# Value weights in tiles of their own, their loads spread over four products, and all refilled low parts on VectorE, in a hybrid attention and retention block

## The chip, the cores and the metric

The kernel runs on one core of one Trainium2 chip, in one launch. The metric is the device time of that core in microseconds (us). TensorE is called PE here, VectorE DVE, ScalarE ACT, GpSimd POOL and SyncE SP. Before the change the median of three runs is 1945.7 us (1945.29 to 1947.35).

## The reference, cut to what matters

A sequence of 2048 rows of 1024 numbers goes through one block. All is computed to float32 accuracy.

```python
h = rms_norm(x, norm_gain[l])
proj = jnp.einsum('bsd,df->bsf', h, w_in[l])
q_a, k_a, v_a, g_a, q_r, k_r, v_r, g_r, m_a, m_r = split_columns(proj)
o_a = chunk_band_attention(q_a, k_a, v_a, rel_bias[l])        # 8 heads, own chunk of 64 and 8 before it
branch_a = jnp.einsum('bsf,fd->bsd', o_a * jax.nn.silu(g_a), w_out_attn[l])
o_r = retention_chunkwise(rotary(q_r), rotary(k_r), v_r, gn_gain[l])   # 8 heads, decay by head
branch_r = jnp.einsum('bsf,fd->bsd', o_r * jax.nn.silu(g_r), w_out_ret[l])
mixed = jax.nn.sigmoid(m_a) * branch_a + jax.nn.sigmoid(m_r) * branch_r
x = x + jnp.einsum('bsd,de->bse', mixed, w_out[l])
return rms_norm(x, final_gain)
```

The change touches the first two lines: the normalized rows, and their product with `w_in`, for the values `v_a` and `v_r` above all.

## The kernel before, in words

**Arithmetic.** Each float32 operand of a matmul is held as two tiles: a high part, which ACT casts (`act.copy`, CAST in the profile), and a low part, the operand less the high part, which DVE or POOL subtracts (TENSOR_TENSOR). A product is then three passes: high by high, high by low, low by high. In the projections, seven products of quarters stand for eight (Strassen's scheme in Winograd's form): `PRODUCTS` lists them with the weight operand (`b11` to `b22`, or a sum `t1` to `t4` of them) and the PSUM bank (x, y, v, z, w). The operands on the side of the rows, `R[0]` to `R[6]` (tile r in the profile, high and low), are made once for each half of the sequence and stay in SBUF.

**Stages.** The sequence is worked in two halves of 1024 rows. Job p0 projects queries, keys and values of the first half (span 0 to about 320 us), in chunks of 256 columns, numbered 0 to 10; g0 projects the gates and fills PE in attention and retention of the first half (to about 750). `reload` then refills R for the second half from DRAM (`cscr`, cs in the profile), where `second_half` has put its parts during p0; p1 does the same chunks (about 755 to 1060), g1 fills attention and retention again (to 1500), and the output projections follow.

**The three kinds of chunk.** `Strassen` has a product of 12 matmuls of 128x512, in four steps of three; the weights are the moving or the stationary operand by the chunk. `Rows` (chunks 3, 5 and 10: values) gives rows by columns, and has 14 half products of 24 matmuls of 128x256, also four steps each. `Front` is the start of p0.

**What sets the order.** The program is written out in one order, which each engine keeps. `dense` yields one step (three matmuls, or six of half size) at a time; `later(n, fn)` puts work n steps later; `prime` prepares an item (a product or a half product) three items ahead: ACT casts the high part (`wh`), and four steps later DVE makes the low part (`wl`). `RAW_LEADS` says how many items ahead of a chunk its weights are loaded: nine and eight. The loads are issued on ACT's queue, in order with ACT's casts. For a `Rows` chunk, line 456 `load(self, js)` issues two loads of 512 KB at lead nine, and four of 256 KB at lead eight, all four in a row.

**Tiles.** `E` gives a tile of 128x512 from one ring (line 113), of 23 tiles in the projections (`E_PROJ`), in program order; it serves projected keys, queries and values until they are put to DRAM, rows of the second half, and in `Rows` the lower weights and `t2`. `raw` is a ring of three tiles of 512 KB for weights. `C` and `t` are rings for sums.

**Other places of the change.** `piece` in `second_half` fetches rows of the second half (xs), scales them on ACT (line 927), and six steps later has PE transpose them (`turn`, tile pst); ACT then scales the transposed tile by the gain, and sums of such tiles go to `cscr`. Line 1154 has PE transpose the keys of the retention (tile trkr_k), fifteen steps after a product's end and more. `refill` (line 974) loads one tile of R's low side with the full number, ACT casts the high part from it, and DVE or POOL subtracts in place; `reload` gives every third of the 28 to POOL:

```python
later(1, lambda k=k, t=t: refill(m, k, cscr[m][k], 8 + 2 * t - 4 * at, pool if t % 3 == 2 else dve))
```

## Time and profile before

| | us |
|---|---|
| median of three runs | 1945.7 (1945.29 to 1947.35) |
| profiled execution | 1943.98 |
| its span | 1942.2 |
| mean granted clock of PE | 0.994 |
| PE busy | 1887.3 (97%) |
| DVE busy | 1355.7 (70%) |
| ACT busy | 930.9 (48%) |
| POOL busy | 898.4 (46%) |

The profile is of one execution. A time line has the start in us from the span's start, the length in us, the engine, the operation, the tiles written and read, and in brackets the idle time ahead of it with what ended it. ACTq is ACT's issuing of transfers. A view by windows has, for each stretch, its length, and busy time (with the number of instructions) of PE, of the weight loads of PE, DVE, ACT and POOL, then PE's granted clock, the share of the DMA engines and GB/s. A line of waits has the tile, what it waited for, the sum in us, how often, and the longest. A line of a tile's view has the number of instructions and the shortest, median and longest in ns. The buffer numbers are left out of tile names. PE's busy time is the quantity that the sum of all matmuls sets; its idle time, and the stretches in which the granted clock is about half, are what else makes up the span.

### The profile page before, as it was taken

What the parts mean: (1) busy time and instruction counts of PE and PEld (TensorE: products, weight loads), DVE (VectorE), ACT (ScalarE), POOL (GpSimd) and SP (SyncE); (2) the same over time, 40 slices, a digit from 0 to 9 for tenths busy, and PEclk for the clock granted to TensorE, in tenths of its full rate; (3) what the DMA queues carried; (4) which work ended last, traced back from release to release, by engine and by line L of the source; (5) the groups of instructions that cost most, each with busy time, mean ns of one, the idle gap of its engine ahead of it and who ended that gap; (6) DMA issues with size and microseconds to landing.
All of it is one profiled execution on the core that took longest, in us unless ns stands there. A gap on an engine that the chain in (4) does not pass through costs nothing. (4 is left out here: it accounts for less than half of the span.)

```text
span 1942.2 us, 31900 instructions
## 1 busy us (share of the span) xinstructions
PE 1887.3 (97%) x10437; PEld 1617.8 (83%) x10437; DVE 1355.7 (70%) x2521; ACT 930.9 (48%) x1931; POOL 898.4 (46%) x742
## 2 busy tenths in 40 slices
PE   7999999999999999999999999999999999999998
PEld 6899879888888887899879888888888878887886
DVE  6969788677756558879788677765555654547665
ACT  7544553666654545343333666664455321223554
POOL 0313525545545566323415544544564114557775
PEclk9999999999999999999999999999999999999999
DMA  6586876565559978575666555555998999977673
GB/s 195 169 279 194 255 263 217 182 192 177 175 156 277 270 239 298 186 257 187 196 222 209 158 166 174 160 155 160 272 274 269 313 357 330 320 261 237 208 240 127
DMA packets 325750, 435.93 MB, mean 224 GB/s; under 512 B 30073, under 2 KB 191377, under 8 KB 325585
## 3 DMA queue, kind: packets, MB, share of 16 engines
q1 hardware_dynamic: 260096, 368.35, 59.3%
q10 hardware_dynamic: 65488, 65.55, 11.2%
q8 instruction: 83, 1.36, 0.3%
q14 instruction: 83, 0.67, 0.1%
HBM read 288.14 MB, written 145.64 MB: 223 GB/s over the span
## 5 line engine op out<-in xcount | busy, mean ns | idle before, releaser
L142 POOL TENSOR_SCALAR pr<-pr,rsum 128x640 f32<-128x640 f32 (+4 forms) x128 | 96.5, 754 | 212.2 <-DVE ptl L142 99.8
L142 PE MATMUL ps_g_z<-r,wh_g 128*128 128x512 f32 x448 | 144.0, 403 | 1.4 <-DVE c_g L142 1.4
L142 PE MATMUL ps_g_x<-r,wh_g 128*128 128x512 f32 x448 | 143.2, 401 | 1.0 <-ACT u_g L142 0.8
L142 DVE CUSTOM_DVE_ANT_0 pr<-wide,bt 128x640 f32<-128x640 f32 (+4 forms) x128 | 94.3, 737 | 61.8 <-PE wide L142 49.7
L142 ACT ACTIVATE pr<-pr,mn 128x640 f32<-128x640 f32 (+4 forms) x128 | 98.0, 766 | 81.9 <-DVE mn L142 81.9
L142 DVE TENSOR_TENSOR ptl<-tp,pth 128x384 fp32r<-128x384 f32 x168 | 96.1, 573 | 41.2 <-ACT pth L142 37.9
L142 ACT CAST pth<-tp 128x384 fp32r<-128x384 f32 x168 | 84.5, 515 | 68.0 <-PE tp L142 64.8
L142 POOL TENSOR_TENSOR l_vr<-vrt,h_vr 128x512 fp32r<-128x512 f32 x32 | 46.8, 1463 | 121.0 <-DMA qrs<-l_q 81.3
L142 POOL TENSOR_TENSOR sl<-sm,sh 128x384 fp32r<-128x384 f32 x64 | 68.9, 1077 | 70.5 <-ACT sh L142 48.2
L142 PEld LDWEIGHTS tp<-ident,pr 128*128 128x128 f32 x560 | 71.1, 140 | 27.4 <-POOL pr L142 2.9
L142 DVE TENSOR_TENSOR sm<-sr,dm 128x384 f32<-128x384 f32 x64 | 35.6, 556 | 82.8 <-DMA dm<-in_dmask_dram 26.3
L142 POOL TENSOR_TENSOR wl_g<-t_g,wh_g 128x512 fp32r<-128x512 f32 x56 | 75.0, 1340 | 39.5 <-ACT wh_g L142 39.2
L142 PE MATMUL po<-pth,va 128*128 128x256 f32 x336 | 92.5, 296 | 0.0
L142 PE MATMUL tp<-ident,pr 128*128 128x128 f32 x560 | 89.3, 272 | 2.9 <-POOL pr L142 1.7
L142 ACT CAST wh_p<-raw_p 128x512 fp32r<-128x512 f32 x99 | 61.3, 621 | 61.7 <-PE ps_p_y L142 23.3
L142 PE MATMUL wide<-ka,qa 128*128 128x384 f32 (+1 forms) x448 | 88.3, 313 | 2.3 <-DVE mn L142 2.1
L142 PEld LDWEIGHTS wide<-ka,qa 128*128 128x128 f32 x448 | 74.5, 188 | 18.9 <-DVE mn L142 9.0
L142 PE MATMUL po<-ptl,va 128*128 128x256 f32 x336 | 88.3, 284 | 1.4
L142 PE MATMUL ps_g_z<-r,wl_g 128*128 128x512 f32 x224 | 88.3, 394 | 0.0
L142 PE MATMUL ps_g_x<-r,wl_g 128*128 128x512 f32 x224 | 88.1, 393 | 0.0
L142 DVE TENSOR_TENSOR wl_p<-raw_p,wh_p 128x512 fp32r<-128x512 f32 x99 | 82.4, 836 | 5.4 <-ACT wh_p L142 5.4
L142 POOL TENSOR_TENSOR t_g<-raw_g,t_g 128x512 f32<-128x512 f32 x56 | 73.7, 1316 | 24.6 <-DVE wl_g L142 10.6
(933 smaller groups left out, 6263.0 us busy)
## 6 DMA issues: line engine op xcount, KB each, us to landing
raw_g<-in_w_in_dram ACTq DMA_DIRECT2D x56, 512.0 KB, 4.3
raw_p<-in_w_in_dram ACTq DMA_DIRECT2D x38, 512.0 KB, 5.8
qa<-qas SPq DMA_DIRECT2D x128, 128.0 KB, 3.1
qr<-qrs SPq DMA_DIRECT2D x128, 128.0 KB, 4.6
vr<-vrs SPq DMA_DIRECT2D x64, 256.0 KB, 5.9
ka<-kas SPq DMA_DIRECT2D x56, 256.0 KB, 3.4
va<-vas SPq DMA_DIRECT2D x40, 256.0 KB, 3.3
kds<-kdt_k SPq DMA_DIRECT2D x32, 256.0 KB, 3.3
```

The lines of the kernel that those rows point to most:

```text
L142: return tc.keep_in_program_order(op(*a, **k))
```

## The change

1. `Rows.load` issues four loads of 512 KB, one each at leads 8, 7, 6 and 5 (`ROW_LEADS`), in the order b12, b11, b22, b21. The lower two go to tiles of a new tag `late` (two of them), for which the ring E has 19 tiles in place of 23: the SBUF taken is the same.
2. The sums of a `Rows` chunk are written over weight tiles: t1 over b11, t3 over b12, t4 over b21; t2 takes a tile of the ring t, so no sum takes an E tile. t1, t2 and t3 are made one item later.
3. At the start, the lower weights of chunk 1 lie in one late tile, s3 is written over a11, and s2 gets E tiles.
4. Rows of the second half are transposed eight steps after their scaling in place of six, the sums made of them two steps later; the keys of the retention are transposed three steps later.
5. All 28 low parts of the refill are made on DVE (19 before).

```diff
-E_PROJ = 23
+E_PROJ = 19
+ROW_LEADS = (8, 7, 6, 5)
@@ Rows
-            for j in range(2) if js is None else js:
-                for h in range(2):
-                    src = w_cols(w_in, self.job.cols[self.c] + T * h, 2, j)
-                    name = f"raw_{self.job.name}_{self.c}_{j}{h}"
-                    if j == 0:
-                        raw = wp.tile([P, 4, T], F32, tag="raw", bufs=RAWS, name=name)
-                        act.dma_start(raw, src)
-                        bs = [raw[:, 2 * kk:2 * kk + 2] for kk in range(2)]
-                    else:
-                        bs = [E(f"{name}_{kk}", shape=(P, 2, T)) for kk in range(2)]
-                        for kk in range(2):
-                            act.dma_start(bs[kk], src[:, 2 * kk:2 * kk + 2])
-                    self.b[f"b{j + 1}{h + 1}"] = bs
-                self.raw.append(j)
-        SUMS_AFTER = {0: ("t1", "t2", 0), 1: ("t1", "t2", 1), 2: ("t3", 0), 3: ("t3", 1), 6: ("t4", 0), 7: ("t4", 1)}
+            for j in range(4) if js is None else js:
+                k, h = ((0, 1), (0, 0), (1, 1), (1, 0))[j]
+                name = f"raw_{self.job.name}_{self.c}_{k}{h}"
+                if k:
+                    raw = epool[0].tile([P, 4, T], F32, tag="late", bufs=2, name=name)
+                else:
+                    raw = wp.tile([P, 4, T], F32, tag="raw", bufs=RAWS, name=name)
+                act.dma_start(raw, w_cols(w_in, self.job.cols[self.c] + T * h, 2, k))
+                self.b[f"b{k + 1}{h + 1}"] = [raw[:, 2 * kk:2 * kk + 2] for kk in range(2)]
+                self.raw.append(raw)
+        SUMS_AFTER = {1: ("t1", "t2", 0), 2: ("t1", "t2", 1), 3: ("t3", 0), 4: ("t3", 1), 6: ("t4", 0), 7: ("t4", 1)}
...
+            into = {"t1": "b11", "t3": "b12", "t4": "b21"}
...
@@ start_up
-        for i in range(2):
-            ch[1].b[f"b2{i + 1}"] = E(f"b2{i + 1}", shape=(P, 4, P))
+        lower = epool[0].tile([P, 4, T], F32, tag="late", bufs=2, name="lower")
+        ch[1].b.update({"b21": lower[:, :, left], "b22": lower[:, :, right]})
-        s3 = [E(f"s3_{k}") for k in range(4)]
+        s3 = a11
-        s2, s1, s4 = a11, a21, a12
+        s2, s1, s4 = [E(f"s2_{k}") for k in range(4)], a21, a12
@@ second_half
-                later(6, lambda: turn(i, f))
+                later(8, lambda: turn(i, f))
-            later(24, first)
-            later(28, second)
-            later(32, third)
+            later(26, first)
+            later(30, second)
+            later(34, third)
@@ refill
-        later(lag + 2, lambda: (low or dve).tensor_tensor(wl, r32(wl), r32(wh), ALU.subtract))
+        later(lag + 2, lambda: dve.tensor_tensor(wl, r32(wl), r32(wh), ALU.subtract))
@@ keys of the retention
-            later(late + 15 + 4 * u, lambda u=u: turn(u))
+            later(late + 18 + 4 * u, lambda u=u: turn(u))
```

On ACT, ahead of chunk 10 of p1: before, two loads and, two instructions later, four in a row (raw_p_10 are the weights of chunk 10, wh_p_9 and h_qa work of chunks 9 and 8, kdt_k of the keys).

```order
L142 ACTIVATE h_qa_2_11972<-ps_p_8_x 128x512
L142 DMA raw_p_10_00_11977<-in_w_in_dram 128x4x256
L142 DMA raw_p_10_01_11979<-in_w_in_dram 128x4x256
L142 CAST wh_p_9_4_11981<-t_p_9_11870 128x512
L142 ACTIVATE h_qa_2_12011<-u_p_8_11933 128x512
L142 DMA raw_p_10_10_0_12014<-in_w_in_dram 128x2x256
L142 DMA raw_p_10_10_1_12015<-in_w_in_dram 128x2x256
L142 DMA raw_p_10_11_0_12018<-in_w_in_dram 128x2x256
L142 DMA raw_p_10_11_1_12019<-in_w_in_dram 128x2x256
L142 CAST wh_p_9_1_12022<-t_p_9_11872 128x512
```

And with the change:

```order
L143 DMA raw_p_10_01_11973<-in_w_in_dram 128x4x256
L143 CAST wh_p_9_1_11975<-t_p_9_11841 128x512
L143 ACTIVATE h_qa_3_12006<-u_p_8_11809 128x512
L143 DMA raw_p_10_00_12009<-in_w_in_dram 128x4x256
L143 CAST wh_p_9_2_12011<-t_p_9_11866 128x512
L143 CAST kdt_k_2_0_0_12019<-trkr_k_2_0_11991 128x4x64
L143 CAST kdt_k_2_0_1_12026<-trkr_k_2_0_11991 128x4x64
L143 COPY u_p_9_12040<-ps_p_9_x 128x512
L143 DMA raw_p_10_11_12046<-in_w_in_dram 128x4x256
L143 CAST wh_p_9_3_12048<-raw_p_9_1_11765 128x512
```

Each load now stands ahead of one cast of chunk 9, and the next load behind that cast.

On PE, in the last product of chunk 8 of p0 (pst are the transposes of scaled rows xs, trkr_k those of the keys, ps_p_8_z the product), before:

```order
L142 MATMUL trkr_k_0_0_3261<-ident,u_p_7_2865 128x128
L142 MATMUL ps_p_8_z<-r_92,wh_p_8_6_3133 128x512
L142 MATMUL ps_p_8_z<-r_93,wh_p_8_6_3133 128x512
L142 MATMUL ps_p_8_z<-r_92,wl_p_8_6_3134 128x512
L142 MATMUL pst_0_1_3290<-ident,xs_0_1_3121 128x128 x4
```

And with the change:

```order
L143 MATMUL ps_p_8_z<-r_93,wh_p_8_6_3113 128x512
L143 MATMUL ps_p_8_z<-r_92,wl_p_8_6_3114 128x512
L143 MATMUL trkr_k_0_0_3267<-ident,xk_0_0_2967 128x128
L143 MATMUL trkr_k_0_0_3267<-ident,u_p_7_2846 128x128
...
L143 MATMUL pst_0_1_3274<-ident,xs_0_1_3103 128x128 x4
L143 MATMUL ps_p_8_z<-r_92,wh_p_8_6_3113 128x512
```

Before, the transposes stand behind the first step of this product; now behind the third, and the keys' transposes, which stood ahead of the product, stand directly ahead of them.

On DVE, at the start of the refill (r are the low parts, c_g_13 a sum of the last chunk of g0, wl_p weights of p1), before:

```order
L142 TENSOR_TENSOR u_g_13_9476<-ps_g_13_v,u_g_13_9384 128x512
L142 TENSOR_TENSOR r_81<-r_81,r_80 128x512
L142 TENSOR_TENSOR wl_g_13_6_9453<-raw_g_13_1_8964,wh_g_13_6_9452 128x512
L142 TENSOR_TENSOR c_g_13_9519<-ps_g_13_z,u_g_13_9476 128x512
L142 TENSOR_TENSOR r_81<-r_81,r_80 128x512
L142 TENSOR_TENSOR wl_p_0_0_9502<-raw_p_0_0_9310,wh_p_0_0_9501 128x512
```

And with the change:

```order
L143 TENSOR_TENSOR r_81<-r_81,r_80 128x512
L143 TENSOR_TENSOR wl_g_13_6_9434<-raw_g_13_1_8945,wh_g_13_6_9433 128x512
L143 TENSOR_TENSOR r_81<-r_81,r_80 128x512
L143 TENSOR_TENSOR c_g_13_9500<-ps_g_13_z,u_g_13_9457 128x512
L143 TENSOR_TENSOR r_81<-r_81,r_80 128x512
L143 TENSOR_TENSOR wl_p_0_0_9483<-raw_p_0_0_9291,wh_p_0_0_9482 128x512
```

The row of r_81 between wl_g_13_6 and c_g_13 is new here; POOL made that low part before. The other eight come in behind, two or more in a row between the low parts of the weights.

## The prediction

> **What bounds the kernel now.** I read first the page's busy times, then PE's waits, then the time lines of the engines that PE waited for.

> ```profile
> span 1942.2 us, 31900 instructions
> PE 1887.3 (97%) x10437; PEld 1617.8 (83%) x10437; DVE 1355.7 (70%) x2521; ACT 930.9 (48%) x1931; POOL 898.4 (46%) x742
> ```

> PE is busy for 1887.3 of 1942.2 us, and the change takes no matmul away. So it can win only from the 54.9 us in which PE stands still, and from time in which PE is busy at a slower clock. The waits (tile, releaser, sum, times, longest) that the change touches are these:

> ```profile
> PE ps_p_y L142 <- ACT wh_p L142: 4.7, 3, 2.8
> PE pst L142 <- ACT xs L142: 2.1, 2, 1.6
> PE ps_g_z L142 <- DVE c_g L142: 1.4, 1, 1.4
> PE ps_p_w L142 <- DVE wl_p L142: 1.4, 2, 1.0
> PE ps_p_z L142 <- DVE wl_p L142: 0.5, 1, 0.5
> PE ps_p_v L142 <- DVE wl_p L142: 0.5, 1, 0.5
> ```

> The view by windows shows the second kind of loss: its PEclk column (the 0.58, 0.57 and 1.00 ahead of the DMA share) says that the clock fell to about half in three of these stretches.

> ```profile
> 254.00:258.00 4.00, 4.00 (x15) 3.08 (x14) 2.99 (x4) 1.04 (x2) 2.96 (x2) 0.58 1.02 339
> 977.00:981.00 4.00, 3.81 (x9) 2.75 (x10) 4.00 (x7) 2.95 (x6) 1.98 (x2) 0.58 0.71 200
> 991.00:995.00 4.00, 4.00 (x11) 2.94 (x10) 3.43 (x8) 3.22 (x8) 0.00 (x0) 0.57 1.06 371
> 781.00:793.00 12.00, 10.09 (x43) 7.38 (x42) 12.00 (x13) 2.89 (x6) 8.52 (x6) 1.00 0.16 56
> ```

> **Part A, the loads of the value weights.** ACT issues them and also casts the weights, in one order. Three bursts of loads hold a cast back (ACTq is the issuing):

> ```profile
> 126.84 6.82 ACTq L142 DMA_DIRECT2D raw_p<-in_w_in_dram  x3
> 133.71 0.62 ACT L142 CAST wh_p<-t_p 128x512 fp32r<-128x512 f32 x1 [8.91 <-DMA raw_p<-in_w_in_dram]
> 254.60 8.78 ACTq L142 DMA_DIRECT2D raw_p<-in_w_in_dram  x4
> 263.42 0.62 ACT L142 CAST wh_p<-t_p 128x512 fp32r<-128x512 f32 x1 [8.38 <-DMA cs<-xs]
> 984.27 5.64 ACTq L142 DMA_DIRECT2D raw_p<-in_w_in_dram  x4
> 989.95 0.62 ACT L142 CAST wh_p<-t_p 128x512 fp32r<-128x512 f32 x1 [7.23 <-DMA raw_p<-in_w_in_dram]
> ```

> Each cast is released by a transfer, after 7.2 to 8.9 us in which ACT did nothing. PE takes up the product at once after the cast:

> ```profile
> 134.38 0.73 PE L142 MATMUL ps_p_y<-r,wh_p 128*128 128x512 f32 x2 [1.20 <-ACT wh_p L142]
> 136.21 0.62 PE L142 MATMUL ps_p_y<-r,wh_p 128*128 128x512 f32 x2
> 136.90 0.62 PE L142 MATMUL ps_p_y<-r,wh_p 128*128 128x512 f32 x2
> 137.60 0.61 PE L142 MATMUL ps_p_v<-r,wh_p 128*128 128x512 f32 x2
> 264.09 0.73 PE L142 MATMUL ps_p_y<-r,wh_p 128*128 128x512 f32 x2 [0.71 <-ACT wh_p L142]
> 267.28 0.61 PE L142 MATMUL ps_p_v<-r,wh_p 128*128 128x512 f32 x2
> 990.62 0.73 PE L142 MATMUL ps_p_y<-r,wh_p 128*128 128x512 f32 x2 [2.76 <-ACT wh_p L142]
> 995.28 0.62 PE L142 MATMUL ps_p_v<-r,wh_p 128*128 128x512 f32 x2
> ```

> A step of three matmuls takes 0.69 us (136.21 to 136.90), so a product of four steps 2.76. The three delayed products take 3.22, 3.19 and 4.66. The loss is wait plus excess, and for the second also the 0.5 of ps_p_v on wl_p, whose low part followed the late cast: 1.20 + 0.46 = 1.7; 0.71 + 0.43 + 0.50 = 1.6; 2.76 + 1.90 = 4.7, where the excess is the half clock. Together **8.0 us**.

> After the change each Rows chunk has four loads of 512 KB, one in every four steps, with casts between them, instead of two and then four in a row. The lead of the casts is three times four steps, 3 x 2.76 = 8.3 us: a single blocked load costs PE nothing until it holds ACT that long. From the landing times, a load may still find its semaphore unfired:

> ```profile
> raw_p<-in_w_in_dram ACTq DMA_DIRECT2D x2, 512.0 KB, 5.7
> krs<-h_k SPq DMA_DIRECT2D x2, 256.0 KB, 6.9
> ```

> The transfers that a load waits for land 5.7 to 6.9 us after their issue (window 975 to 992), below 8.3 but not far below, and ACT has other casts to do. So I take the three waits as gone (-8.0) and leave one new wait of the size of the first, +1.7; the bounds for what remains are 0 (no wait) and 8.0 (all three as before).

> The smaller pieces here: 24 loads in place of 36 in all; the sums t1, t2 and t3 one half product (four steps) later on DVE, still one ahead of their cast, which itself runs three ahead; three of the four sums written over a weight tile. None lies on the path as long as the lead of 8.3 us holds; if it goes, the price is that of a wait above. In the start the low half of chunk 1's weights gets a tile of its own, and s3 is written over a11: I put +0.1 there, between 0 and 0.3.

> **Part B, transposes two steps later.** In the first half PE reaches the transposes of scaled rows before ACT is done with them:

> ```profile
> 252.12 0.62 PE L142 MATMUL pst<-ident,xs 128*128 128x128 f32 x2 [1.63 <-ACT xs L142]
> 253.56 0.85 PE L142 MATMUL ps_p_z<-r,wh_p 128*128 128x512 f32 x2
> 257.19 0.38 PE L142 MATMUL trkr_k<-ident,xk 128*128 128x128 f32 x1
> 252.73 0.69 ACT L142 ACTIVATE xs<-xs,rs 128x128 f32<-128x128 f32 x2
> ```

> Between 252.12 - 1.63 = 250.5 and 253.56 PE did four short transposes, and the three steps from 253.56 took 3.63 us instead of 3 x 0.69 = 2.07, at the clock of 0.58 shown above. Now two of these steps stand ahead of the transposes, so PE gets there at 250.5 + 2 x 0.69 = 251.9. ACT ends the last scaling at 252.73 + 0.69 = 253.4 as it is; one more cast now stands ahead of it, about 0.3, so 253.7. With the transposes PE is through at about 253.9, one step is left, and the place of 257.19 is reached at about 254.6: a gain of **2.6**, which I take as 2.5. If the clock falls all the same, the 1.56 of excess stays and the gain is 0.9; if nothing waits, it is up to 4.2. The other fifteen groups of transposes (four pieces of four tiles) stand in no wait of the list, and lie two steps later at no cost.

> The keys' transposes three steps later touch the third slow stretch, which starts with a wait on c_p:

> ```profile
> 977.13 0.78 PE L142 MATMUL ps_p_z<-r,wh_p 128*128 128x512 f32 x2 [1.20 <-DVE c_p L142]
> ```

> DVE is busy in all of 977 to 981 and behind with c_p; the change takes none of the work ahead of c_p away. I take **0**, with a gain of 2 (half a clock for four us) at best.

> **Part C, the 28 low parts of the refill.** Nine go from POOL to DVE.

> ```profile
> L142 POOL TENSOR_TENSOR r<-r,r x9: 1721/1735/2989, 745.9 to 786.1; 128x512 fp32r<-128x512 f32 x9
> 747.02 1.18 DVE L142 SCALAR_TENSOR_TENSOR rt<-rt,rt 32x512 f32<-32x512 f32 x1
> 751.97 0.67 DVE L142 TENSOR_TENSOR c_g<-ps_g_z,u_g 128x512 f32<-128x512 f32 x1
> 752.57 0.67 DVE L142 TENSOR_TENSOR r<-r,r 128x512 fp32r<-128x512 f32 x1
> 783.26 1.77 DVE L142 TENSOR_TENSOR r<-r,r 128x512 fp32r<-128x512 f32 x1
> 757.00:769.00 12.00, 10.43 (x45) 7.99 (x44) 12.00 (x9) 8.32 (x17) 11.92 (x8) 1.00 1.05 394
> 790.80 0.50 PE L142 MATMUL ps_p_w<-r,wl_p 128*128 128x512 f32 x1 [0.99 <-DVE wl_p L142]
> ```

> A DVE operation of this size takes 0.67, and the next starts 0.60 after it (751.97 to 752.57). The one at 783.26 took 1.77; from 757 to 769, with POOL busy all the time (11.92 of 12), DVE got through only 9 operations in 12 us. So nine more cost DVE 9 x 0.60 = 5.4, and nine POOL operations less free it of up to 9 x (1.77 - 0.67) = 9.9: DVE comes out up to 4.5 lighter, and if its slow operations had another cause than POOL, 5.4 heavier. I take the first, since the slow ones lie where POOL is busy. Between 781 and 793 DVE is busy without a break and PE loses 12 - 10.09 = 1.91, in the three waits for wl_p of the list (1.4 in two and 0.5). Those go: **-1.9**. Ahead of c_g one more low part stands (+0.60), while POOL's first at 745.9 no longer slows the 1.18 operation at 747.02 (-0.50): **+0.1** on that wait of 1.4. Sum -1.8, from -3 (c_g too) to +5.4.

> **Sum.** -8.0 + 1.7 + 0.1 - 2.5 + 0 - 1.8 = -10.5 us. The profiled execution took 1943.98 us (1942.2 of span, 1.8 around it), so 1933.5; the median of 1945.7 lies 1.7 above that, so the forecast is **1935**.

> **The rivals.** First, the slow clock may be set by something else than the gap. [...] The rows speak against it: 0.57 and 0.58 stand right behind gaps of 2.76 and (transposes apart) 2.1 us, and waits of 1.20 (at 134) and 1.4 (for c_g) brought none. Were the half clocks to stay in their places, A would lose 1.9 and B 1.6 of their gain: 1935 + 3.5 = 1938.5.

> Second, the loads block as before: with four issues in four products instead of two places, the semaphores may be as late, and ACT's casts queue behind each. For it speaks that transfers land only after 5.7 to 6.9; against it that between two loads there are now 2.76 us and casts of 0.62. Then A is worth nothing, B 0.9, C 1.8: 1945.7 - 2.7 = 1943.

> Third, slower: the ring of 512-wide tiles shrinks from 23 to 19. Its tiles carry keys, queries and values until their puts have landed, and in the chunks of the retention's keys those need 6.9 us. A tile is taken again four allocations earlier; where that is before the landing, ACT or DVE stalls at the first write. From 8.3 us on such a stall reaches PE, at 8.0 / 3 = 2.7 us each. In the six chunk passes of keys (three in each half) that is +16 - 10.5 = +5.5: 1951. Against it: the six tiles of a Rows chunk that filled this ring are gone from it.

> Fourth, better: the wait on c_p ends sooner too, and B pays in full: 1935 - 2 - 1.7 - 1.2 (c_g) = 1930.

> **How the numbers follow.** The forecast has 0.46, the clock rule 0.10, loads that still block 0.20, the ring 0.13, the better case 0.11. The range runs from 1929 (under the better case) to 1947, which leaves out most of the ring's and little else. 0.2% is 3.9 us, about what can be told from no change here: faster means under 1941.8, slower over 1949.6. The forecast, the clock rule and the better case make 0.67, of which a little goes to "same" for waits I have not foreseen, as does a little of the ring's: faster 0.66, same 0.21, slower 0.13.

> **What would show it.** Right: no ACT idle of 7 us before wh_p in chunk 10, the wait ps_p_y on wh_p at most 1.2 instead of 4.7, PEclk near 1.00 where 991 to 995 was, pst on xs under 1.6 with no half clock behind it, DVE's r operations at 0.6 to 0.7 and no wl_p wait in the refill. Wrong: a wait on wh_p or h_k, of any chunk, over 2 us with ACT released by a put or a load; DVE still without a break at 798; PE's idle time still near 55 us.

## The result, and the profile after

The changed kernel takes 1934.51 us in the median of five runs (1928.76 to 1937.13), against 1945.7 before (five runs by now, 1942.84 to 1947.35). The ratio is 0.994, with a 95% interval of 0.9923 to 0.9957. It was timed twice more below: 0.9941 (0.9928 to 0.9954) and 0.9939 (0.9925 to 0.9954). The ratios are estimated from all runs of both kernels, so they differ a little from the quotient of two medians. Two runs, one of e0 (its profiled one, 1957.26 us at a granted clock of 0.926) and one of the kernel before beside it (4806.09 us), were slow and are left out of every number, so e0 has no row in the table below. The changed kernel is faster by 0.6%, and the forecast was 1935. Several of the forecast's steps were still wrong.

The page of the profiled execution (1934.51 us) has

```profile
span 1932.7 us, 31908 instructions
PE 1877.7 (97%) x10437; PEld 1614.5 (84%) x10437; DVE 1353.5 (70%) x2530; ACT 931.1 (48%) x1931; POOL 885.1 (46%) x733
```

The span is 9.5 us shorter and PE's busy time 9.6, with the same matmuls; its idle time is 55 us as before. Fewer stretches at half clock (one in place of five) make up most of that, by an estimate of 1.6 to 1.9 us for each from the lines before (last section), and the waits that went were replaced by others. Of PE's waits, these answer to those shown before:

```profile
PE ps_g_z L143 <- DVE c_g L143: 2.7, 2, 1.5
PE pst L143 <- DVE kdt_k L143: 2.3, 1, 2.3
PE ps_p_z L143 <- DVE c_p L143: 2.2, 1, 2.2
PE ps_p_y L143 <- DVE wl_p L143: 0.9, 1, 0.9
PE ps_p_w L143 <- DVE wl_p L143: 0.9, 1, 0.9
```

The wait of ps_p_y on wh_p, 4.7 us, is gone from the list altogether. The wait of pst on xs (2.1) is gone too, but pst now waits 2.3 for kdt_k. The wait for c_p has grown from 1.2 to 2.2, and a wait of ps_p_y for wl_p is new. Of the two waits for c_g, the one of 1.5 is that of the refill; the other, 1.2 at 695.7, lies outside the places of the change.

ACT's time line ahead of chunk 10 of the second half, where it was held for 7.2 us before:

```profile
979.49 0.38 ACTq L143 DMA_DIRECT2D raw_p<-in_w_in_dram  x1
982.66 0.37 ACTq L143 DMA_DIRECT2D raw_p<-in_w_in_dram  x1
986.65 0.38 ACTq L143 DMA_DIRECT2D raw_p<-in_w_in_dram  x1
987.07 0.62 ACT L143 CAST wh_p<-raw_p 128x512 fp32r<-128x512 f32 x1 [2.31 <-DMA krs<-l_k]
988.16 0.37 ACTq L143 DMA_DIRECT2D raw_p<-in_w_in_dram  x1
```

The third load still waits for the keys' put, as the prediction feared, but for 2.31 us, which the lead of the casts covers. The longest hold by a load after the change stands ahead of chunk 3 of the second half, and no wait of PE on wh_p follows it:

```profile
806.49 0.62 ACT L143 CAST wh_p<-t_p 128x512 fp32r<-128x512 f32 x1 [5.38 <-DMA raw_p<-in_w_in_dram]
```

To see where the time went, I set the start of the same matmul in a trace against its start in the trace before, and took the difference over five stretches (starts in us of the span before; the median of twelve matmuls at each end; negative is time won). Apart from the ratio, each row is one profiled execution.

| | ratio to before, 95% interval | 60 to 115 | 115 to 140 | 140 to 320 | 745 to 800 | 960 to 1000 |
|---|---|---|---|---|---|---|
| after | 0.9940 (0.9923, 0.9957) | +1.8 | -1.9 | -1.9 | -1.2 | -6.5 |
| e10 after again | 0.9939 (0.9925, 0.9954) | +2.0 | -1.9 | -2.1 | +0.8 | -5.1 |
| e1 low parts alone | 0.9988 (0.9976, 1.0000) | 0.0 | +0.9 | -0.7 | -1.8 | -0.3 |
| e2 loads alone | 0.9974 (0.9963, 0.9985) | +1.7 | -1.9 | -1.7 | +0.5 | -6.3 |
| e3 lags alone | 0.9991 (0.9978, 1.0005) | +0.1 | +0.7 | -1.3 | +0.5 | -0.8 |
| e4 loads in pairs | 0.9965 (0.9952, 0.9977) | +4.0 | -1.9 | -2.3 | -1.2 | -4.5 |
| e5 keys at 15 | 0.9952 (0.9937, 0.9968) | +1.7 | -1.9 | -2.9 | +2.1 | -6.3 |
| e6 spread alone | 0.9979 (0.9966, 0.9991) | +0.9 | -1.9 | -1.4 | +1.4 | -6.3 |
| e7 rows at 10 | 0.9928 (0.9915, 0.9941) | +1.8 | -1.9 | -3.6 | -1.6 | -4.9 |
| e9 rows at 10 again | 0.9937 (0.9923, 0.9951) | +1.8 | -1.9 | -3.4 | -1.8 | -4.9 |
| e8 rows at 10, lower parts later | 0.9937 (0.9919, 0.9955) | +1.8 | -1.9 | -3.3 | -1.8 | -6.5 |

The stretches hold, in this order, chunk 2 with the loads and sums of chunk 3; the burst of chunk 5; the transposes at 250 with the burst of chunk 10, up to the end of p0, behind the last transposes of rows in every kernel; the refill; the wait for c_p with the burst of chunk 10 of the second half.

### The profile page after: what moved, and what is told of

Same layout as the page of the kernel before. It is cut to its first block, busy times and chain, and to the rows that moved or that the text cites. A ratio compares the mean times of both kernels' runs of the same rounds, so it can differ in the third digit from the quotient of the medians.

```text
span 1932.7 us, 31908 instructions
## 1 busy us (share of the span) xinstructions
PE 1877.7 (97%) x10437; PEld 1614.5 (84%) x10437; DVE 1353.5 (70%) x2530; ACT 931.1 (48%) x1931; POOL 885.1 (46%) x733
## 5 line engine op out<-in xcount | busy, mean ns | idle before, releaser
L143 ACT CAST wh_p<-raw_p 128x512 fp32r<-128x512 f32 x111 | 68.0, 619 | 49.9 <-PE ps_p_y L143 15.5
L143 PEld LDWEIGHTS ps_g_x<-r,wh_g 128*128 128x128 f32 x448 | 75.8, 189 | 10.7 <-ACT u_g L143 2.5
## 6 DMA issues: line engine op xcount, KB each, us to landing
raw_g<-in_w_in_dram ACTq DMA_DIRECT2D x56, 512.0 KB, 5.1
raw_p<-in_w_in_dram ACTq DMA_DIRECT2D x50, 512.0 KB, 5.7
vr<-vrs SPq DMA_DIRECT2D x64, 256.0 KB, 5.4
ka<-kas SPq DMA_DIRECT2D x56, 256.0 KB, 3.2
va<-vas SPq DMA_DIRECT2D x40, 256.0 KB, 3.3
kds<-kdt_k SPq DMA_DIRECT2D x32, 256.0 KB, 3.3
```

Source lines behind the costliest of these rows:

```text
L143: return tc.keep_in_program_order(op(*a, **k))
```

## The experiments

The theory going in was the prediction's: bursts of loads hold ACT's casts (part A), transposes come too early (B), and DVE is slowed by POOL in the refill (C). The rival to each stands in the expectations.

### The three parts, each alone

e1 is the kernel before, with

```diff
-        later(lag + 2, lambda: (low or dve).tensor_tensor(wl, r32(wl), r32(wh), ALU.subtract))
+        later(lag + 2, lambda: dve.tensor_tensor(wl, r32(wl), r32(wh), ALU.subtract))
```

> The kernel before with one edit: all 28 low parts of the refill on VectorE. By the prediction's part C the three waits for wl_p between 781 and 793 us (1.9 us of idle PE) go and the wait for c_g stays at about 1.5: PE idle between 749 and 799 us falls from 4.9 to about 3, the profiled span is about 1.2 to 1.8 us shorter, and the ratio to before is 0.9985 to 1.000. The rival, that the slow VectorE operations have another cause than GpSimd, expects VectorE 5.4 us later in the refill and the time 3 to 5 us longer (ratio over 1.0015), with operations on r still at 1.7 us in 757 to 793.

Measured: median 1939.45 against 1943.12 for the kernel before on the same chip, ratio 0.9988. The tile view of r (count, then shortest, median and longest in ns), before and in e1, and a window of e1's refill:

```profile
L142 DVE TENSOR_TENSOR r<-r,r x19: 669/1182/1786, 749.6 to 791.9; 128x512 fp32r<-128x512 f32 x19
```

```profile
L142 DVE TENSOR_TENSOR r<-r,r x28: 670/678/1789, 752.3 to 793.6; 128x512 fp32r<-128x512 f32 x28
```

```profile
781.00:793.00 12.00, 12.00 (x54) 9.79 (x53) 12.00 (x16) 4.99 (x9) 6.31 (x4) 1.00 0.10 37
```

The median low part on DVE costs 678 ns in place of 1182, though there are nine more: with POOL's operations most of the slow ones went. In e1 PE has no gap from 781 to 793, where 1.91 us were lost. The refill is 1.8 us shorter, and the rival (DVE 5.4 us later) falls. PE's idle time from 749 to 799, expected to fall from 4.9 to about 3, is 3.9: near 759 ps_p_x now waits 1.68 us for u_p, where it waited 0.89 before. Part C below comes back to this wait.

e2 is the changed kernel, with the lags of before (6, 24, 28, 32 and 15 steps) and every third low part of the refill on POOL again.

> The changed kernel with the loads, tiles, sums and start as changed, but the transposes at their old lags and a third of the refill's low parts on GpSimd as before. If the loads carry the gain (part A: 8.0 less about 1.3 that the profile after shows lost near 92 us by the later sums), the ratio to before is 0.9955 to 0.9975 and PE waits for wh_p in chunk 10 nowhere over 0.5 us; the waits at 250 us (pst) and in the refill stay as before. The rival, that the lags or the low parts carry a good part of the gain, expects a ratio of 0.998 to 1.000.

Measured: 1938.03, ratio 0.9974, at the upper end of what was expected if the loads carry the gain, and clear in the stretches. No wait on wh_p is left, and at the three bursts 1.9, 1.7 and 6.3 us are won. What is lost between 60 and 115 is there too, +1.7; here (and in e5) it stands as a wait of 1.16 us of trkr_k for c_p, which DVE makes.

e3 is the kernel before with the lags of the change:

```diff
-                later(6, lambda: turn(i, f))
+                later(8, lambda: turn(i, f))
-            later(late + 15 + 4 * u, lambda u=u: turn(u))
+            later(late + 18 + 4 * u, lambda u=u: turn(u))
```

(and the sums behind `turn` 2 steps later.)

> The kernel before with one edit: rows of the second half transposed 2 steps later with the sums behind them, keys 3 steps later. By the prediction's part B the wait of pst on xs and the half clock behind it go: 2.5 us less, ratio 0.9985 or lower. By what the profile after shows (PE waits 2.3 us in the transposes of rows for kdt_k, the low parts of the keys, because the keys' later transposes hold the PSUM tile that the rows' take next) the gain at this place is under 1 us, a wait for kdt_k of about 2 us stands there, a half clock behind it is as likely as before, and the ratio is 0.999 to 1.001.

Measured: 1940.73, ratio 0.9991, with an interval that reaches from a gain of 0.2% to none. The waits of e3 show the exchange:

```profile
PE pst L142 <- DVE kdt_k L142: 2.3, 1, 2.3
PE ps_p_z L142 <- DVE c_p L142: 2.2, 1, 2.2
```

The first was not there before, and the second was 1.2; the waits of pst on xs (2.1) and of trkr_k (0.64, ahead of c_p's) are gone. The lags alone trade waits for others of the same length.

### What in the loads does it: their spread, or their number

e4 is the changed kernel with its four loads issued in two pairs:

```diff
-        sooner = {at - lead: (ch, [j]) for ch, at in begins.items()
-                  for j, lead in enumerate(ROW_LEADS if isinstance(ch, Rows) else RAW_LEADS)}
+        sooner = {at - lead: (ch, [2 * j, 2 * j + 1] if isinstance(ch, Rows) else [j]) for ch, at in begins.items()
+                  for j, lead in enumerate(RAW_LEADS)}
```

> The changed kernel with one edit: the four loads of 512 KB of a chunk of values are issued in two pairs, at leads nine and eight, in place of one at each of the leads 8, 7, 6 and 5. If issuing in a row is what holds ScalarE's casts (part A), the waits of ps_p_y on wh_p come back in chunks 5 or 10 with ScalarE released by a transfer after 5 us and more, and the time is 3 to 8 us over the changed kernel's: ratio to before 0.996 to 0.999. The rival, that the tiles of their own (no slot of the ring to wait for) and the 4 loads in place of 6 are enough, expects no wait on wh_p over 0.5 us and a ratio of 0.993 to 0.9955.

Measured: 1936.22, ratio 0.9965. ACT's time line of e4 at the three places of before, and ACT's and PE's in chunk 2:

```profile
132.65 2.90 ACTq L143 DMA_DIRECT2D raw_p<-in_w_in_dram  x2
135.59 0.62 ACT L143 CAST wh_p<-t_p 128x512 fp32r<-128x512 f32 x1 [6.74 <-DMA vas<-vat]
259.98 3.55 ACTq L143 DMA_DIRECT2D raw_p<-in_w_in_dram  x2
263.57 0.62 ACT L143 CAST wh_p<-t_p 128x512 fp32r<-128x512 f32 x1 [4.65 <-DMA krs<-l_k]
981.58 3.16 ACTq L143 DMA_DIRECT2D raw_p<-in_w_in_dram  x2
984.78 0.62 ACT L143 CAST wh_p<-t_p 128x512 fp32r<-128x512 f32 x1 [4.62 <-DMA qas<-h_qa]
```

```profile
72.32 0.58 ACT L143 CAST h_ka<-ps_p_(1, 1)_883 128x512 fp32r<-128x512 f32 x1 [6.33 <-PE ps_p_w L143]
73.48 0.73 PE L143 MATMUL ps_p_y<-r,wh_p 128*128 128x512 f32 x2 [1.24 <-ACT wh_p L143]
```

Both sides are half right. The pairs hold ACT for 4.6 to 6.7 us where the six loads held it for 7.2 to 8.9, and at the three places of before PE no longer waits on wh_p. But in chunk 2, where the loads of chunk 3 cost nothing before, the wait on wh_p is new: ACT stands still for 6.33 us until the last load of a pair is issued, at 71.85, and PE then waits 1.24 for the next cast. 4.0 are lost from 60 to 115 in place of 1.8.

So a hold under 8.3 us is not free everywhere. Counted from the moment at which ACT stops to the one at which PE has nothing left, the lines shown give 8.4 and 8.3 us at the first two bursts before (124.80 to 133.18, 255.04 to 263.38), but 5.1 at the third (982.72 to 987.86) and 6.2 here (65.99 to 72.24). At the third burst the cast ahead of the loads had itself come after a wait of 1.47 us for DVE. So its hold, the shortest of the three at 7.23 us, cost the most, 2.76.

e6 goes the other way: the kernel before, its six loads (four of them into tiles of the ring) spread over leads 8, 7, 6 and 5.

```diff
-            for j in range(2) if js is None else js:
-                for h in range(2):
+            for n in range(4) if js is None else js:
+                j, h = ((0, 1), (0, 0), (1, 1), (1, 0))[n]
...
+                  for j, lead in enumerate((8, 7, 6, 5) if isinstance(ch, Rows) else RAW_LEADS)}
```

> The kernel before with one edit: the six loads of a chunk of values (two of 512 KB, four of 256 KB in tiles of the ring) are spread over leads 8, 7, 6 and 5, the halves of a lower quarter one after the other. Tiles, sums and lags as before. If spreading alone frees the casts (part A), the waits of ps_p_y on wh_p go, with no late sums near 92 us, and the ratio to before is 0.995 to 0.997. The rival, by which fewer loads and tiles outside the ring carry half of it (in pairs, the four loads held ScalarE for 4.6 to 6.7 us, the six before for 7.2 to 8.9), expects ScalarE held for 3 us and more at the lower quarters and a wait on wh_p over 1 us in one of the chunks: ratio 0.997 to 0.999.

Measured: 1938.39, ratio 0.9979. At the three bursts it wins as much as the change does (-1.9, and -6.3 between 960 and 1000). ACT is held at the lower quarters there for 3.38 us and then for 4.43, before a cast at 996.24 for which PE waits 0.78 us (ps_p_w on wh_p). Later PE waits for a low part. ACT's time line at the first of the two, then PE's:

```profile
988.80 2.34 ACTq L142 DMA_DIRECT2D raw_p<-in_w_in_dram  x2
991.19 0.62 ACT L142 CAST wh_p<-raw_p 128x512 fp32r<-128x512 f32 x1 [3.38 <-DMA krs<-l_k]
```

```profile
1010.13 0.39 PE L142 MATMUL ps_p_y<-wl_p,r 128*128 128x256 f32 x1 [1.35 <-DVE wl_p L142]
```

So spreading alone takes the three waits on wh_p away, and so do four loads in pairs, each with one smaller wait on wh_p at another place (0.8 in e6, 1.2 in e4). The kernels whose loads are both fewer and spread (after, e2, e5 and e7 to e10) have none. That the time did not follow comes from elsewhere: +1.4 in the refill, where a stretch at half clock lies, +1.9 from 800 to 960, and +2.9 from 1000 to 1100, 0.78 and 1.35 of it in the two waits just named. Why wl_p is late there was not separated.

### The transposes at 250 us

After the change, PE reaches the transposes of rows at 248.0 and finds their PSUM tile in use. First PE's time line, then DVE's:

```profile
250.38 0.99 PE L143 MATMUL pst<-ident,xs 128*128 128x128 f32 x4 [2.34 <-DVE kdt_k L143]
```

```profile
249.71 0.42 DVE L143 TENSOR_TENSOR kdt_k<-trkr_k,kdt_k 128x256 fp32r<-128x256 f32 x1
```

kdt_k is the low part of the transposed keys, read from PSUM. Rows and keys share a ring of four PSUM tiles, and the keys' tile, filled three steps later, is read later by DVE. e5 puts the keys back to 15 steps, and the rows stay at 8:

> The changed kernel with one edit: the keys are transposed 15 steps later as before, in place of 18; the rows of the second half keep their 8. If the keys' later transposes hold the PSUM tile that the rows' take next, the wait of pst for kdt_k (2.3 us near 250) falls under 0.7, no half clock follows, and the time is 2 to 4 us under the changed kernel's (ratio to before 0.992 to 0.9945); the waits of trkr_k on DVE sums (0.6 and 1.2 us) come back. The rival, that the rows' own lag of 8 is what puts them there, expects the 2.3 us unchanged and the ratio of the changed kernel.

Measured: 1933.83, ratio 0.9952: no better than the changed kernel. PE's time line of e5:

```profile
249.26 0.63 PE L143 MATMUL pst<-ident,xs 128*128 128x128 f32 x4 [1.14 <-DVE kdt_k L143]
251.27 0.33 PE L143 MATMUL trkr_k<-ident,xk 128*128 128x128 f32 x1 [0.69 <-ACT xs L143]
```

The wait for kdt_k is halved (1.14; I had expected under 0.7), and part of what was won is spent on the next waits, trkr_k's and then pst's for xs (0.7 and 1.4): the stretch to 320 us gives 2.9 in place of 1.9 and 2.1. So the keys' lag explains half of it. e7 gives the rows two more steps instead (10, with the sums behind them at 28, 32 and 36):

> The changed kernel with one edit: rows of the second half are transposed 10 steps after their scaling in place of 8, the sums behind them 2 steps later; keys stay at 18. If the wait for kdt_k is a matter of who comes first to the PSUM tile, VectorE is done with it at about 250.1 us and PE comes two steps (1.4 us) later: the wait falls from 2.3 to about 1, and the one for xs stays under 0.5, 1 to 3 us less than the changed kernel (ratio 0.9925 to 0.995). The rival, that the wait moves on to the next transposes, expects 2 us and more in pst or trkr_k within the 20 us that follow and no gain.

Measured: 1929.16, ratio 0.9928. PE's time line of e7:

```profile
250.54 0.63 PE L143 MATMUL pst<-ident,xs 128*128 128x128 f32 x4 [0.97 <-DVE kdt_k L143]
252.88 0.33 PE L143 MATMUL trkr_k<-ident,xk 128*128 128x128 f32 x1 [0.32 <-ACT xs L143]
254.76 0.60 PE L143 MATMUL pst<-ident,xs 128*128 128x128 f32 x4
```

0.97 in place of 2.34, the last transposes wait for nothing, and no half clock follows: 3.6 us are won from 140 to 320 in place of 1.9 and 2.1. Up to 275 us it was 5.0 (2.6 after, 4.1 in e10). Part of that is lost again, 0.8 of it in two waits that the changed kernel does not have there:

```profile
294.07 0.38 PE L143 MATMUL ps_p_v<-wl_p,r 128*128 128x256 f32 x1 [0.18 <-DVE wl_p L143]
300.71 0.39 PE L143 MATMUL ps_p_z<-wl_p,r 128*128 128x256 f32 x1 [0.63 <-DVE wl_p L143]
```

The second comparison, side by side:

> The changed kernel with rows of the second half transposed 10 steps after their scaling, again, beside the changed kernel: if the 2.5 us that its profile won near 250 us are lasting (a wait of 1.0 in place of 2.3, and no half clock), it is 1 to 3 us under the changed kernel; if the first comparison was chance, both have the same median within 1 us.

> The changed kernel again, for the comparison with the run above: ratio to before 0.993 to 0.996. In its profile PE waits 2.2 to 2.4 us for kdt_k near 250 us, whether or not a half clock follows; by the grid seen so far one follows where PE is busy for less than 1.5 of the 3.41 us of a stretch of the grid, and none where it is busy for more than 1.95.

> The changed kernel again, beside the three below on the same chip, for a narrower interval. Ratio to before 0.993 to 0.996. Half-clock stretches may stand elsewhere than in its first profile, since a wait of 2.2 us brought one in one profile and none in another; the waits on wh_p in the chunks of values stay away, and pst waits for kdt_k for about 2.3 us near 250 us.

Measured: e9 1930.38 (0.9937), e10 1931.8 (0.9939), e0 1931.24 (0.9941). The place is better by about 1.5 us in both profiles of the ten steps (-3.6 and -3.4); in the whole time the medians differ by 2.1 us in the first comparison and 1.4 in the second, within the intervals. So ten steps are better at their place, and not shown to be faster in all. The expectation of e10, that no half clock follows where PE is busy for more than 1.95 us of a stretch, did not hold: in e10 itself one follows a stretch from 1416 us with 2.00 (last section).

e8 adds to e7 the low parts of the refill two steps later (`lag + 4` for `lag + 2`).

> The changed kernel with two edits: rows of the second half transposed 10 steps after their scaling (as in the run before this one), and all low parts of the refill two steps later. One low part less then stands ahead of c_g on VectorE (0.6 us each), and the first one is no longer ahead of its predecessor sum: the wait of ps_g_z for c_g falls from 1.5 to about 0.3. If VectorE's backlog behind it is not needed earlier, this is worth 1 us on top of the run without it (ratio 0.992 to 0.994). The rival, that the first products of the second half then wait for the low parts of r themselves, expects new waits of ps_p_x on r of 1 us and more near 756 and a ratio of 0.994 or more.

Measured: 1929.03, ratio 0.9937. In its waits

```profile
PE ps_g_z L143 <- DVE c_g L143: 0.9, 1, 0.9
```

0.9 in place of 1.5 (not 0.3), no wait on r in its place, and 1.8 us won in the refill, as without the edit: the gain at c_g was given back before 800.

## Why the prediction was right, and where it was not

**Part A, the loads: right in its sum, wrong in its bound.** The terms were 1.7, 1.6 and 4.7 us. Chunk 5 gave 1.9 in every kernel with spread or fewer loads. Chunk 10 of the first half gave 1.7 in e2, where the transposes are as before. Chunk 10 of the second half gave 4.9 in e7 and e9, where nothing else was won in that stretch. Sum 8.5 against 8.0. That the loads are held by earlier transfers is what ACT's releasers show, before and in e4. The bound was wrong, though: a load does not cost PE nothing until it holds ACT for 8.3 us. The third burst of the prediction's own lines (7.23 us, a wait of 2.76) and e4 (6.33 us, a wait of 1.24) both lie under it. What told in these four cases is the hold against what was left of the lead at that place: 8.91 us against 8.4, 8.38 against 8.3, 7.23 against 5.1, and 6.33 against 6.2 in e4.

**The residue of +1.7: right in size, wrong in kind.** I left it for a load that still blocks. Loads do still hold ACT (5.38 us at most), but none makes PE wait. And the sentence that the later sums lie off the path as long as the lead holds is wrong. Time lines after, ACT and then PE:

```profile
90.70 0.62 ACT L143 CAST wh_p<-t_p 128x512 fp32r<-128x512 f32 x1 [3.09 <-DVE t_p L143]
```

```profile
92.44 0.39 PE L143 MATMUL ps_p_y<-wl_p,r 128*128 128x256 f32 x1 [0.91 <-DVE wl_p L143]
```

The cast of t2 waits 3.09 us for the sum, which DVE now makes one half product later, behind the keys' rotary work. The stretch costs 1.7 to 2.0 in all kernels with the late sums (4.0 in e4, with its wait on wh_p), 0.0 and 0.1 in e1 and e3, and 0.9 in e6, whose sums are early but whose loads are late. So the late sums are the likely cause of most of it; no run has them alone. The +0.1 for the start came out as it was put, 0.1 from 20 to 60.

**Part B, the transposes: the step failed.** I let PE come 1.4 us later and find the rows all but scaled. They were, but the PSUM tile was not free, for which I had not asked: the other edit of this part, the keys three steps later, takes it away. The wait moved from xs (1.63) to kdt_k (2.34). After, the clock fell behind it as before. In e10 it did not fall, so 1.9 us more than in e2 were won up to 275 us, but most of that was lost again in a wait of the next transposes:

```profile
280.58 1.21 PE L143 MATMUL pst<-ident,xs 128*128 128x128 f32 x4 [1.87 <-ACT xs L143]
```

So against e2 (1.7 from 140 to 320) this part gave 0.2 after and 0.4 in e10, in place of 2.5; even the 0.9 that the prediction had for a clock that falls all the same was not reached. Ten steps reach 1.9 (3.6 less e2's 1.7); the upper bound of 4.2 for the case in which nothing waits was reached nowhere.

**The wait on c_p: a term of 0, right but for the clock.** The later keys drew two waits together, 2.2 in place of 0.64 at trkr_k and 1.2 for c_p; after, e3, e4 and e7 to e10 all have 2.2. Of the 6.5 us between 960 and 1000 after, 1.6 is a slow stretch that fell away; in e4, e7, e9 and e10 it is there.

**Part C, the refill: right in size in e1 (1.8 forecast, 1.8 measured), with a term left out.** The three waits for wl_p went, and c_g stayed at 1.5. After, the gain was 1.2, with a wait of 0.9 for wl_p left:

```profile
757.00:769.00 12.00, 10.16 (x44) 7.78 (x43) 12.00 (x12) 8.34 (x17) 8.42 (x6) 1.00 1.05 396
781.00:793.00 12.00, 11.10 (x49) 8.79 (x48) 11.98 (x17) 3.39 (x7) 3.54 (x3) 1.00 0.19 58
```

DVE gets through 12 operations from 757 to 769 in place of 9, and PE loses 0.9 in place of 1.91 from 781 to 793.

The term left out is the wait of ps_p_x for u_p. First PE before and in e10, then ACT in e10:

```profile
759.36 0.73 PE L142 MATMUL ps_p_x<-r,wh_p 128*128 128x512 f32 x2 [0.89 <-ACT u_p L142]
759.93 0.73 PE L143 MATMUL ps_p_x<-r,wh_p 128*128 128x512 f32 x2 [2.79 <-ACT u_p L143]
```

```profile
757.74 0.63 ACT L143 ACTIVATE u_g<-u_g 128x512 f32<-128x512 f32 x1 [1.84 <-DVE u_g L143]
```

DVE makes u_g between the low parts, one more of which now stands ahead of it; ACT waits for u_g and reaches u_p later. The prediction asked for this only at c_g. The wait is 0.7 to 0.9 in the four kernels that leave a third of the low parts on POOL (before, e2, e3, e6), and 1.2 to 2.8 in the eight with all of them on DVE. In e10 and e5, where it is 2.8, half-clock stretches follow at 761 us, and the refill takes 0.8 and 2.1 us more than before. So part C is worth between 1.8 and less than nothing, and the sum depends on this wait.

**The sum.** By the runs: -8.5 + 1.8 + 0.1 - 0.3 - 0.7 = -7.6 us (part B as the mean of after and e10, part C as that of e1, after and e10), for -10.5 forecast. The three comparisons of medians gave 11.2, 11.8 and 12.0 us, each known to about 3. So some 4 us of the measured gain stand in none of the terms, and where they come from is not shown. That 1935 lies within 1 us of the measured 1934.51 is therefore in part luck: parts B and C gave 1.0 in place of 4.3. The single parts add up the same way: 0.26% (e2), 0.12% (e1) and 0.09% (e3) make 0.47%, for 0.6% measured together, each known to about 0.12%.

**The rivals.** The loads did not block on; the ring of 19 tiles cost nothing that shows. The first rival (the clock rule among the chances), that the slow clock is set by something else than the gap and the half clocks stay in their places, was half right. The one at 991 us went with the wait in every kernel with the changed loads or e6's, and stayed in e1 and e3; the one at 250 us stayed after the change, though not in e10. What stood ahead of them is in the last section.

**The signs.** The wait on wh_p went, as the signs of being right had it. But a wait for wl_p is left in the refill, a half clock still stands behind pst, and PE's idle time, which the prediction named as a sign of being wrong if it stayed near 55 us, is 55.0 (51.9 in e10).

## What to carry to other kernels

Where an engine both issues transfers and does the work that feeds the bottleneck, read the longest time that it is held, and set it against what is left of the lead of that work at that place, not against the full lead: here holds of 6.3 and 7.2 us cost PE a wait under a lead of 8.3. Fewer issues in a row and issues spread between the work both shortened the holds: from 7.2 to 8.9 us to 4.6 to 6.7 with four in pairs (e4), to 5.4 at most with four spread (after), and to 3.4 and 4.4 with six spread (e6). When a consumer is moved later, ask for everything that it needs, its output tile too: here the transposes waited as long for a PSUM tile (2.3 us) as before for their input (2.1), in good part because a neighbour in the same ring had been moved later with them. When work moves to an engine, look at everything that stands behind it in that engine's order, not only at the wait that it is meant to cure. Where the bottleneck's clock falls after a wait, the price of a wait is uncertain by the price of the slow stretch (1.6 to 1.9 us here), and a change of a few us is to be read place by place and not from two spans.

## What the runs showed of the hardware

```profile
974.19:977.60 3.41, 1.57 (x8) 0.76 (x7) 3.38 (x6) 0.58 (x2) 0.59 (x1) 1.00 0.41 156
977.60:981.02 3.42, 3.36 (x8) 2.48 (x8) 3.42 (x6) 2.36 (x6) 2.00 (x2) 0.50 0.76 208
```

```profile
247.10:250.51 3.41, 1.07 (x6) 0.60 (x5) 3.38 (x7) 2.21 (x5) 0.48 (x1) 1.00 0.13 50
250.51:253.92 3.41, 3.41 (x11) 2.83 (x11) 1.71 (x5) 3.41 (x11) 2.59 (x2) 0.50 0.82 288
970.72:974.13 3.41, 1.68 (x8) 1.06 (x6) 3.34 (x4) 0.00 (x0) 1.83 (x2) 1.00 0.20 76
974.13:977.55 3.42, 2.98 (x15) 2.38 (x16) 2.87 (x7) 3.10 (x8) 1.36 (x1) 1.00 0.36 128
```

```profile
972.71:976.12 3.41, 1.28 (x6) 0.74 (x4) 3.34 (x5) 0.08 (x1) 1.43 (x1) 1.00 0.20 77
976.12:979.54 3.42, 3.38 (x8) 2.74 (x9) 2.87 (x6) 3.42 (x8) 1.76 (x1) 0.50 0.44 155
```

After and in e10 the same kernel has the same wait for c_p, 2.17 us. In the one it lies across the border of two stretches (1.68 busy) and the clock stays; in the other it lies within one but for 0.04 us (1.28 busy) and the clock halves. Over the twelve profiles, away from their ends, every stretch at full clock with under 1.5 us of PE busy was followed by a slow one, and none with over 2.1 was. In between both happened: before, a slow one follows 1.57 us (the first row above), and after, at full clock again, none follows 1.57 (the stretch from 1769.44). The sum in the stretch tells more than one gap: in the first row above, waits of 0.64 and 1.20 us together left 1.57 busy, and the next stretch was slow, while a single wait of 2.17 us after brought no slow one. What in the chip makes the clock fall was not shown.

A slow stretch costs 1.6 to 1.9 us, estimated from two places before: three steps from 253.56 took 3.63 us for 2.07, and the product of 990.62 took 4.66 for 2.76. The kernel before has five of them in its profile, the changed one has one in its first profile (after) and four in its second (e10). By that price three more would be some 5 us. Yet the two executions of the changed kernel have spans of 1932.7 and 1932.9 us: in the second PE is busy for 3.3 us more (1881.0) and idle for 3.1 less. So the number of slow stretches alone does not tell the time, and that the 8.4 us between the lowest and the highest of the changed kernel's first five runs come from them was not shown: only profiled executions tell the stretches.
